# Differential attention in one encoder kernel: both components' scores in one product with the keys on a diagonal, and the product with V turned so that queries lie on partitions

## The chip, the cores and the metric

One core of one Trainium2 chip runs the whole program. The metric is the device time of one execution in microseconds (us); the time of a kernel is the median of its runs.

## What is computed

The reference is a two-layer encoder in float32 on 256 positions of width 2048: a conformer convolution, a gated FFN with a 3-tap convolution, a differential attention, a second FFN, with RMS norms between. The change lies in the attention. For each of 16 heads it does, cut to what matters:

```python
q = q.reshape(B, S, N_HEADS, 2, HEAD_DIM) * (HEAD_DIM ** -0.5)   # two components of 64 channels
k = k.reshape(B, S, N_HEADS, 2, HEAD_DIM)
v = v.reshape(B, S, N_HEADS, 2 * HEAD_DIM)                       # 128 channels
s = einsum('bqhcd,bkhcd->bhcqk', qb, k)                          # scores of each component c
s = where(allowed, s + bias, -inf)                               # by blocks of 128 queries
p = softmax(s)
a = p[:, :, 0] - lam * p[:, :, 1]
o = einsum('bhqk,bkhe->bqhe', a, v)
o = rmsnorm(o, subln_g) * (1 - lambda_init)                      # over the 128 channels of a head
return o.reshape(B, S, D_MODEL) @ w_o
```

The first 128 queries see only the first 128 keys, so one of the four 128 x 128 blocks of a head is never computed.

## The kernel before, in words

**Layout.** Activations lie with channels on the 128 partitions and the 256 positions along the row. A weight block of 128 x 1024 is loaded by SP's queue (`load_w`, L140), split by ACT into a rounded part `hi` (L150) and by DVE or POOL into the rest `lo` (L152). A projection (`pair`, L215) multiplies `hi` with both parts of the activations in one product of 512 columns (L238, at the last channel block L236) and `lo` with the rounded part in one of 256 columns (L239, L235). So a projection is 32 such pairs of products, and PE never stops for anything else. The tile names `pp`, `s`, `t`, `o` are PSUM buffers: two each of `pp` and `s`, one each of `t` and `o`.

**Steps.** The program is a list of steps, one per weight block. `at(n, f)` hangs a piece of work n steps later. A scheduler that builds the program then sets the order on each engine, so the place in the list is where a piece may begin to stand, not where it stands. Each engine works through its own list strictly in order.

**Attention before** (`attention`, L782). Every four heads a group of V products comes first (`v_group`, 96 products of 512 columns, L807 to L809); then each head has its q and k projection, and after it the pieces of that head, each in between the projections of later heads:

- `qk_post` (L826): q and k are summed, normed and each split into `hi` and `lo`; POOL copies the first 128 columns of both, unsplit.
- `scores` (L845): the two components lie on partitions 0 to 63 and 64 to 127. The first query block is two products of 64 rows in full float32 (L851); the second is three split products per component, also of 64 rows (L854). Then the softmax on DVE and ACT (L861 to L873).
- `transp` (L876): three transposes bring keys onto partitions (L879); the first key block is split in two (`AT`), the second kept whole.
- `av` (L885): V is stationary, so the result has channels on partitions: three products of 256 columns and one of 128 in full float32 (L888 to L891).
- `subln` (L899) sums the squares over partitions with products by ones (L286), DVE and POOL make the reciprocal root (L297, L298); `subln2` (L906) spreads it over the partitions with two products (L292), DVE multiplies, and the result is split for the last projection.

After the heads come the projections by `w_o`; the last channel block of the first two is held back until the last head is done.

A full float32 product appears as two records in the trace, a split one as one record.

Of the kernel before, what the change touches and what calls it, by code (L numbers as in the profile page):

```python
# [8 lines left out]
F32 = mybir.dt.float32  # L9
F32R = mybir.dt.float32r  # L10
# [4 lines left out]
P = 128  # L15
S = 256
# [45 lines left out]
class Builder:  # L62
# [683 lines left out]
    def attn_setup(self):  # L746
# [32 lines left out]
        for i in range(2):  # L779
            self.AT.append((self.ph2.tile([P, 2, S], F32R, name=f"at{i}"), self.ph2.tile([P, P], F32, name=f"au{i}")))  # L780

    def attention(self, nin, nout):  # L782
# [3 lines left out]
        V, U, O, BM = {}, {}, {}, {}  # L786

        def v_group(g, off):
            box = {}
            n = c.VK * 512  # L790
            for k0 in range(0, KT, c.VK):
# [3 lines left out]
                def mm(hi, lo, k0=k0):  # L795
                    if k0 == 0:
                        box["ps"] = self.pp.tile([P, 2, 512], F32, tag="pp", name=self.nm("pp"))
                    if k0 == 0:
                        for e in range(4):
                            V[4 * g + e] = self.act_tile()  # L800
# [10 lines left out]
                def post():  # L811
                    for e in range(4):
                        h = 4 * g + e
                        v = V[h][1]
                        U[h] = self.ph2.tile([P, P], F32, tag="vu", name=self.nm("vu"), bufs=6)
                        src = [box["ps"][:, t, e * P:(e + 1) * P] for t in range(2)]
                        r = nin["rc"]
                        nc.scalar.activation(v[:, 0, :P], src[0], AF.Copy, scale=r[:, 0:1])
                        nc.vector.scalar_tensor_tensor(v[:, 1, :P], src[0], r[:, 0:1], v[:, 0, :P].bitcast(F32), ALU.mult,
                                                       ALU.subtract)  # L820
                        nc.scalar.activation(U[h], src[1], AF.Copy, scale=r[:, 1:2])
# [4 lines left out]
        def qk_post(h, ps):  # L826
            t = self.summed(ps)
            nc.vector.tensor_tensor(t, t, nin["rstd"].unsqueeze(1).to_broadcast([P, 2, S]), ALU.mult)
            q = self.b2("Y", F32R)
            k = self.b2("Y", F32R)  # L830
            qk = self.b1("G").rearrange("p (x s) -> p x s", x=2)
# [5 lines left out]
            self.at(2, lambda: scores(h, q, k, qk))  # L837
# [7 lines left out]
        def scores(h, q, k, qk):  # L845
            bm = BM.pop(h)
            ps = [self.psx("s", [P, 2, S]) for _ in range(2)]

            comp = [slice(cc * HD, (cc + 1) * HD) for cc in range(2)]
            for cc, d in enumerate(comp):  # L850
                nc.tensor.matmul(ps[cc][:, 0, :P], qk[d, 0, :], qk[d, 1, :], start=True, stop=True)  # L851
            for i, (qh, kh) in enumerate(((0, 0), (0, 1), (1, 0))):
                for cc, d in enumerate(comp):
                    nc.tensor.matmul(ps[cc][:, 1, :], q[d, qh, P:], k[d, kh, :], start=(i == 0), stop=(i == 2))  # L854
            sm = self.sm.tile([P, 2, 8], F32, tag="smx", name=self.nm("smx"), bufs=2)
            at_ = self.b2("A")
            for t in range(2):
                nk = P * (t + 1)
                s = self.b2("Z")[:, :, :nk]
                for cc in range(2):  # L860
                    nc.vector.scalar_tensor_tensor(s[:, cc, :], ps[cc][:, t, :nk], HD ** -0.5, bm[:, S - nk:], ALU.mult,  # L861
                                                   ALU.add)
# [13 lines left out]
        def transp(h, at_):  # L876
            ps = self.psx("t", [P, 2, S])
            for kt, t in ((0, 0), (0, 1), (1, 1)):
                nc.tensor.transpose(ps[:, kt, t * P:(t + 1) * P], at_[:, t, kt * P:(kt + 1) * P], self.ident)  # L879
            A, B = self.AT[h % 2]  # L880
            self.split_act(A, ps[:, 0, :])
            nc.scalar.copy(B, ps[:, 1, P:])
            self.at(3, lambda: av(h, A, B))

        def av(h, A, B):  # L885
            po = self.psx("t" if h == H - 1 else "o", [P, S])
            v = V[h][1]
            nc.tensor.matmul(po, v[:, 0, :P], A[:, 0, :], start=True, stop=False)  # L888
            nc.tensor.matmul(po[:, P:], U.pop(h), B, start=False, stop=False)
            nc.tensor.matmul(po, v[:, 0, :P], A[:, 1, :], start=False, stop=False)  # L890
            nc.tensor.matmul(po, v[:, 1, :P], A[:, 0, :], start=False, stop=True)  # L891
            self.free([V.pop(h)])
            o = self.b1("O")
            nc.scalar.copy(o, po)
            sq = self.b1("O")
            nc.scalar.activation(sq, po, AF.Square)
            self.at(2, lambda: subln(h, o, sq))

        def subln(h, o, sq):  # L899
            ps = self.psx("t" if h == H - 1 else "o", [P, 4])  # L900
            self.chan_sums(ps, [sq])
            rc = self.c2()
            self.rsqrt_cols(rc, ps[:, 0:4:2], 1.0 / P)
            self.at(2, lambda: subln2(h, o, rc))

        def subln2(h, o, rc):  # L906
            rr = self.psx("t" if h == H - 1 else "o", [P, S])
            self.rows(rr, rc)
            nc.vector.tensor_tensor(o, o, rr, ALU.mult)
            O[h] = self.act_tile()  # L910
            self.split_act(O[h][1], o, self.sg)
# [156 lines left out]
```

## Time and profile before

| | before |
|---|---|
| median of 3 runs | 2267.56 us (2267.46 to 2270.97) |
| the profiled execution, device time | 2268.81 us |
| its span in the profile | 2267.0 us |
| PE busy | 2219.3 us, 98% of the span |
| PE weight loads | 1944.0 us, 86% |
| DVE busy | 1635.4 us, 72% |
| ACT busy | 1205.2 us, 53% |
| POOL busy | 292.0 us, 13% |
| DMA | 417.55 MB, mean 184 GB/s |
| granted clock of PE, whole run | 0.99 of 2.4 GHz |

Engines in the profile: PE multiplies, PEld is its weight load, DVE and ACT work on tiles, POOL is GpSimd, SP issues loads. Matmuls are pipelined, so a record's duration holds latency that overlaps the next one: what a product costs PE is the distance from its start to the next start. That is how PE's prices are read below.

### The profile page before, as it was taken

What the parts mean: (1) busy time and instruction counts of PE and PEld (TensorE: products, weight loads), DVE (VectorE), ACT (ScalarE), POOL (GpSimd) and SP (SyncE); (2) the same over time, 40 slices, a digit from 0 to 9 for tenths busy, and PEclk for the clock granted to TensorE, in tenths of its full rate; (3) what the DMA queues carried; (4) which work ended last, traced back from release to release, by engine and by line L of the source; (5) the groups of instructions that cost most, each with busy time, mean ns of one, the idle gap of its engine ahead of it and who ended that gap; (6) DMA issues with size and microseconds to landing.
All of it is one profiled execution on the core that took longest, in us unless ns stands there. A gap on an engine that the chain in (4) does not pass through costs nothing.

```text
span 2267.0 us, 34768 instructions
## 1 busy us (share of the span) xinstructions
PE 2219.3 (98%) x13382; PEld 1944.0 (86%) x13382; DVE 1635.4 (72%) x2491; ACT 1205.2 (53%) x1788; POOL 292.0 (13%) x197
## 2 busy tenths in 40 slices
PE   5999899999999999999999999999999999999998
PEld 5999788788888888888888888888888888888887
DVE  4788675877767777677777677767777677676774
ACT  4333554655545555555555555555555455554554
POOL 4788510100000000000110101110000000000002
PEclk8999999999999999999999999999999999999999
DMA  6677357755555555555555545455555555555552
GB/s 234 196 215 212 116 192 161 241 185 193 187 191 188 187 186 189 191 187 186 195 167 167 167 161 168 151 196 185 189 186 187 192 187 187 191 187 188 188 189 98
DMA packets 126007, 417.55 MB, mean 184 GB/s; under 512 B 14416, under 2 KB 26704, under 8 KB 125840
## 3 DMA queue, kind: packets, MB, share of 16 engines
q1 hardware_dynamic: 113040, 400.42, 53.9%
q10 hardware_dynamic: 11520, 11.45, 2.0%
q0 software_dynamic: 1280, 3.46, 1.3%
q8 instruction: 105, 1.72, 0.3%
q14 instruction: 62, 0.51, 0.1%
HBM read 407.55 MB, written 7.72 MB: 183 GB/s over the span
## 4 chain that ended last, share of the span: by engine, by line
PE 94%; DMA 2%; DVE 1%; POOL 0%; ACT 0%; issue 0%; ACTq 0%; POOLq 0%; DVEq 0%
PE pp L238 48%; PE pp L239 25%; PE pp L229 7%; PE pp L236 4%; PE pp L235 2%; PE pp L807 1%; PE pp L809 1%; PE pp L808 1%; DMA raw<-in_w_up_dram 1%; PE s L498 1%; DMA R<-ud 0%; PE o L292 0%; PE s L854 0%; DMA ud<-cpad 0%; PE t L498 0%; PE o L286 0%
## 5 line engine op out<-in xcount | busy, mean ns | idle before, releaser
L238 PE MATMUL pp<-act,hi 128*128 128x512 f32 x3902 | 1382.6, 396 | 6.2 <-DVE act L645 3.1
L239 PE MATMUL pp<-act,lo 128*128 128x256 f32 x3902 | 1097.5, 281 | 0.0
L150 ACT CAST hi<-raw 128x1024 fp32r<-128x1024 f32 x752 | 788.0, 1049 | 529.2 <-PE pp L238 180.9
L152 DVE TENSOR_TENSOR lo<-raw,hi 128x1024 fp32r<-128x1024 f32 x686 | 846.0, 1234 | 301.0 <-ACT hi L150 299.0
L238 PEld LDWEIGHTS pp<-act,hi 128*128 128x128 f32 x3902 | 733.8, 188 | 167.4 <-DVE act L645 3.4
L239 PEld LDWEIGHTS pp<-act,lo 128*128 128x128 f32 x3902 | 741.1, 190 | 10.3
L238 PE MATMUL pp<-actb,hi 128*128 128x512 f32 x856 | 306.8, 396 | 1.7 <-ACT hi L150 1.7
L239 PE MATMUL pp<-actb,lo 128*128 128x256 f32 x856 | 240.8, 281 | 0.8 <-DVE lo L152 0.8
L333 POOL TENSOR_TENSOR ssq<-ssq,Z 128x512 f32<-128x512 f32 x24 | 35.6, 1483 | 1516.6 <-ACT Z L329 1516.5
L229 PE MATMUL pp<-act,hi 128*128 128x256 f32 x1088 | 203.4, 289 | 9.1 <-ACT act L279 6.2
L238 PEld LDWEIGHTS pp<-actb,hi 128*128 128x128 f32 x856 | 160.7, 188 | 40.1 <-ACT hi L150 2.0
L229 PEld LDWEIGHTS pp<-act,hi 128*128 128x128 f32 x1088 | 173.7, 196 | 15.6 <-ACT act L279 6.2
L152 POOL TENSOR_TENSOR lo<-raw,hi 128x1024 fp32r<-128x1024 f32 x66 | 158.3, 2414 | 57.6 <-ACT hi L150 52.1
L239 PEld LDWEIGHTS pp<-actb,lo 128*128 128x128 f32 x856 | 162.0, 189 | 1.3 <-DVE lo L152 1.1
L229 PE MATMUL pp<-act,lo 128*128 128x256 f32 x544 | 156.5, 288 | 1.7 <-POOL lo L152 1.5
L382 ACT COPY E<-pp 128x512 f32<-128x512 f32 x109 | 63.9, 586 | 171.5 <-PE pp L236 163.8
L268 DVE TENSOR_TENSOR E<-pp,E 128x512 f32<-128x512 f32 x104 | 71.8, 691 | 105.1 <-ACT E L266 104.9
L266 ACT COPY E<-pp 128x512 f32<-128x512 f32 x104 | 60.8, 585 | 162.7 <-PE pp L236 162.5
L704 DVE SCALAR_TENSOR_TENSOR Y<-fpad,prm,Y 128x256 f32<-128x256 f32 x352 | 146.8, 477 | 0.0
L384 DVE TENSOR_TENSOR x<-pp,x 128x512 f32<-128x512 f32 x101 | 69.7, 690 | 89.5 <-ACT E L382 89.0
L701 ACT ACTIVATE Y<-fpad,prm 128x256 f32<-128x256 f32 x176 | 96.3, 595 | 47.5 <-DVE fpad L697 47.5
L229 PEld LDWEIGHTS pp<-act,lo 128*128 128x128 f32 x544 | 106.7, 196 | 2.1 <-POOL lo L152 1.7
(222 smaller groups left out, 1841.9 us busy)
## 6 DMA issues: line engine op xcount, KB each, us to landing
raw<-in_w_up_dram SPq DMA_DIRECT2D x352, 512.0 KB, 3.9
raw<-in_w_down_dram SPq DMA_DIRECT2D x176, 512.0 KB, 3.9
raw<-in_w_in_dram SPq DMA_DIRECT2D x64, 512.0 KB, 4.4
raw<-in_w_qk_dram SPq DMA_DIRECT2D x64, 512.0 KB, 3.6
raw<-in_w_out_dram SPq DMA_DIRECT2D x32, 512.0 KB, 3.9
raw<-in_w_v_dram SPq DMA_DIRECT2D x32, 512.0 KB, 3.6
raw<-in_w_o_dram SPq DMA_DIRECT2D x32, 512.0 KB, 3.6
R<-ud ACTq DMA_DIRECT2D x52, 132.0 KB, 4.6
```

The source lines that it names most:

```text
L150: nc.scalar.copy(hi[:, :n], raw[:, :n])
L152: ins = eng.tensor_tensor(lo[:, :n], raw[:, :n], hi[:, :n].bitcast(F32), ALU.subtract)
L229: nc.tensor.matmul(ps[:, 0:S], w[:, kk, cs], xt[:, x, :], start=(k == first and n == 0), stop=(k == last and n == 2))
L236: nc.tensor.matmul(*main, start=False, stop=True)
L238: nc.tensor.matmul(*main, start=(k == first), stop=False)
L239: nc.tensor.matmul(*corr, start=False, stop=False)
L266: nc.scalar.copy(cs, ps[:, :, S:])
L268: nc.vector.tensor_tensor(t, ps[:, :, 0:S], cs, ALU.add)
L382: nc.scalar.copy(cs, ps[:, :, S:])
L384: nc.vector.tensor_tensor(x, ps[:, :, 0:S], x, ALU.add)
L701: nc.scalar.activation(y[:, j, :], u[:, j, FK - 1:], AF.Identity, scale=self.col("fw", ch * FK + FK - 1), bias=self.col("fb", ch))
L704: nc.vector.scalar_tensor_tensor(y[:, j, :], u[:, j, q:q + S], self.col("fw", ch * FK + q), y[:, j, :], ALU.mult, ALU.add)
```

## The change

- **Scores.** q keeps its 128 rows (both components). The keys of component 0 go to rows 0 to 63 of a first half-row of `KD`, those of component 1 to rows 64 to 127 of a second half-row; the rest of `KD` is zero, set once by four memsets (L786 of the new text) in `attn_setup`. One product then gives both components side by side. There are three split products for each query block, of 256 and of 512 columns (L863), all with 128 rows. The full-float32 products of the first block and POOL's copy go; the keys' split is now two copies and two subtractions on 64 partitions (L840, L842).
- **Mask and bias** are added for both components in one DVE instruction per query block (two instead of four, L869).
- **V** is kept whole in float32, two heads to a tile; the two evictions of a pair of heads cover both (ACT and DVE one each).
- **Product with V.** The transposed probabilities are copied whole (one ACT copy) and are stationary: three full-float32 products of 128 columns (L898) give queries on partitions.
- **Norm.** Queries are on partitions, so ACT squares and sums along the row (two instructions with accumulation, L903), and DVE scales by a column (two, L910). The products by ones and the spreading products go; two transposes bring the result back (L916).

```diff
+        self.KD = [self.ph2.tile([P, 2, S], F32R, name=f"kd{i}") for i in range(2)]
+        for t in self.KD:
+            for cc in range(2):
+                d = slice((1 - cc) * HD, (2 - cc) * HD)
+                nc.vector.memset(t[d, cc, :].bitcast(F32), 0.0)
...
-            self.split_act(k, t[:, 1, :])
-            nc.gpsimd.tensor_copy(qk, t[:, :, :P])
+            for i in range(2):
+                for cc in range(2):
+                    d = slice(cc * HD, (cc + 1) * HD)
+                    if i == 0:
+                        nc.scalar.copy(self.KD[0][d, cc, :], t[d, 1, :])
+                    else:
+                        nc.vector.tensor_tensor(self.KD[1][d, cc, :], t[d, 1, :], self.KD[0][d, cc, :].bitcast(F32),
+                                                ALU.subtract)
...
-            for cc, d in enumerate(comp):
-                nc.tensor.matmul(ps[cc][:, 0, :P], qk[d, 0, :], qk[d, 1, :], start=True, stop=True)
-            for i, (qh, kh) in enumerate(((0, 0), (0, 1), (1, 0))):
-                for cc, d in enumerate(comp):
-                    nc.tensor.matmul(ps[cc][:, 1, :], q[d, qh, P:], k[d, kh, :], start=(i == 0), stop=(i == 2))
+            for t in range(2):
...
+                nk = P * (t + 1)
+                ps.append(self.psx("s", [P, 2, nk]))
+                for i, (x, k) in enumerate(((0, kh), (0, kl), (1, kh))):
+                    nc.tensor.matmul(ps[t], q[:, x, t * P:(t + 1) * P], k[:, :, :nk], start=(i == 0), stop=(i == 2))
...
+            A = self.AT[h % 2]
+            nc.scalar.copy(A, ps)
+            self.at(3, lambda: av(h, A))
...
+            po = self.psx("o", [P, 2, P])
+            v = V[h // 2][1][:, h % 2, :].rearrange("p (t c) -> p t c", t=2)
+            for i, (kt, t) in enumerate(((0, 0), (0, 1), (1, 1))):
+                nc.tensor.matmul(po[:, t, :], A[:, i, :], v[:, kt, :], start=(kt == 0), stop=(kt == t))
...
+            for t in range(2):
+                nc.scalar.activation(sq[:, t * P:(t + 1) * P], po[:, t, :], AF.Square, accum_out=sums[:, t:t + 1])
+            self.rsqrt_cols(rc, sums, 1.0 / P)
+            self.at(1, lambda: scaled(h, po, rc))
...
+        def scaled(h, po, rc):
+            o = self.b1("O").rearrange("p (t c) -> p t c", t=2)
+            for t in range(2):
+                nc.vector.tensor_scalar(o[:, t, :], po[:, t, :], rc[:, t:t + 1], None, ALU.mult)
+            self.at(2, lambda: back(h, o))
...
+        def back(h, o):
+            ps = self.psx("t", [P, S])
+            for t in range(2):
+                nc.tensor.transpose(ps[:, t * P:(t + 1) * P], o[:, t, :], self.ident)
+            O[h] = self.act_tile()
+            self.split_act(O[h][1], ps, self.sg)
```

The scheduler sets the order anew. Three places of it follow, as the built program lists them; a number behind a name is a buffer's, and "x2" means that the row stands twice. Outside the attention the order changes at one more place only, the first two `w_out` projections after the convolution.

PE, the scores of the fourth head, before: `s` are the two score buffers, `G` POOL's copy, `Y` the split q and k, `pp` the projection between which they stand.

```order
L851 MATMUL s_11805<-G_11735 128x128
L851 MATMUL s_11806<-G_11735 128x128
L292 MATMUL o_11773<-ident,c_11702 128x128 x2
L854 MATMUL s_11805<-Y_11734,Y_11733 128x256
L854 MATMUL s_11806<-Y_11734,Y_11733 128x256
L854 MATMUL s_11805<-Y_11734,Y_11733 128x256
L854 MATMUL s_11806<-Y_11734,Y_11733 128x256
L854 MATMUL s_11805<-Y_11734,Y_11733 128x256
L854 MATMUL s_11806<-Y_11734,Y_11733 128x256
L809 MATMUL pp_11747<-hi_11679,act_10704 128x512
```

and in the change, where L888 is a transpose and L813 to L815 are the V products:

```order
L888 MATMUL t_11767<-ident,A_11630 128x128
L863 MATMUL s_11772<-kd_3983,Y_11709 128x256
L863 MATMUL s_11776<-kd_3983,Y_11709 128x512
L814 MATMUL pp_11722<-lo_11679,act_10763 128x512
L888 MATMUL t_11767<-ident,A_11630 128x128 x2
L815 MATMUL pp_11722<-hi_11678,act_10763 128x512
L863 MATMUL s_11772<-kd_3984,Y_11709 128x256
L863 MATMUL s_11772<-kd_3983,Y_11709 128x256
L863 MATMUL s_11776<-kd_3984,Y_11709 128x512
L863 MATMUL s_11776<-kd_3983,Y_11709 128x512
```

The products with the keys' rounded part stand first, the other four after a few products of the projection.

DVE, at the end of the convolution, where the layer norm's last channel block is made (L523, L569) and its sums are read (L611): one piece of the difference.

```order
 L519 SCALAR_TENSOR_TENSOR pp_2952<-cpad_252,cprm,pp_2952 128x256 x2
 L523 TENSOR_TENSOR O_2983<-pp_2952,O_2983 128x256
+L786 MEMSET kd_3983 64x256 x2
+L786 MEMSET kd_3984 64x256 x2
 L569 TENSOR_TENSOR act_2966<-pp_2952,O_2983 128x256
 L611 SCALAR_TENSOR_TENSOR mom<-o_2989,early 128x4
```

The four memsets that zero `KD` have been moved ahead to this place.

PE, the end of the held projections by `w_o`, before: `pp_14382` is the first of them, whose buffer the next projection `pp_14690` takes over.

```order
L236 MATMUL pp_14382<-act_14373,hi_14219 128x512
L236 MATMUL pp_14467<-act_14373,hi_14445 128x512
L235 MATMUL pp_14467<-act_14373,lo_14446 128x256
L236 MATMUL pp_14467<-act_14373,hi_14445 128x512
L236 MATMUL s_14552<-act_14373,hi_14530 128x512
L236 MATMUL s_14553<-act_14373,hi_14530 128x512
L238 MATMUL pp_14690<-act_11905,hi_14548 128x512
```

and in the change, where the two are `pp_14186` and `pp_14494`:

```order
L236 MATMUL pp_14186<-act_14177,hi_14039 128x512
L236 MATMUL pp_14271<-act_14177,hi_14249 128x512
L235 MATMUL pp_14271<-act_14177,lo_14250 128x256
L236 MATMUL pp_14271<-act_14177,hi_14249 128x512
L238 MATMUL s_14357<-act_14156,hi_14334 128x512
L239 MATMUL s_14357<-act_14156,lo_14335 128x256
L235 MATMUL s_14356<-act_14177,lo_14335 128x256
L236 MATMUL s_14356<-act_14177,hi_14334 128x512
L235 MATMUL s_14357<-act_14177,lo_14335 128x256
L236 MATMUL s_14357<-act_14177,hi_14334 128x512
L238 MATMUL pp_14494<-act_11701,hi_14352 128x512
```

Four more products stand between the end of the first projection and the product that takes its buffer.

## Rows read from the trace of the kernel before

**Rows 1.** The page: engines' busy time; the chain that ended last, by engine.

```profile
PE 2219.3 (98%) x13382; PEld 1944.0 (86%) x13382; DVE 1635.4 (72%) x2491; ACT 1205.2 (53%) x1788; POOL 292.0 (13%) x197
...
PE 94%; DMA 2%; DVE 1%; POOL 0%; ACT 0%; issue 0%; ACTq 0%; POOLq 0%; DVEq 0%
```

**Rows 2.** Attention's stretch: length, busy of PE, PEld, DVE, ACT, POOL, clock, DMA.

```profile
1103.10:1454.40 351.30, 351.23 (x2016) 297.84 (x2015) 250.22 (x514) 195.08 (x399) 36.41 (x33) 1.00 0.51 166
```

**Rows 3.** Timeline of PE, stage marks: start, duration, engine, line, operation, tiles.

```profile
1118.63 0.39 PE L808 MATMUL pp<-lo,act 128*128 128x512 f32 x1
...
1125.91 0.39 PE L238 MATMUL pp<-act,hi 128*128 128x512 f32 x1
...
1137.21 0.39 PE L238 MATMUL pp<-act,hi 128*128 128x512 f32 x1
...
1176.73 0.40 PE L807 MATMUL pp<-hi,act 128*128 128x512 f32 x1
...
1256.44 0.40 PE L807 MATMUL pp<-hi,act 128*128 128x512 f32 x1
```

**Rows 4.** Timeline of PE around the sums by ones and the product with V.

```profile
1206.49 0.50 PE L286 MATMUL o<-ones,O 128*128 128x2 f32 x4
...
1207.17 0.28 PE L239 MATMUL pp<-act,lo 128*128 128x256 f32 x1
...
1210.47 0.28 PE L888 MATMUL o<-at,act 128*128 128x256 f32 x1
...
1211.05 0.39 PE L238 MATMUL pp<-act,hi 128*128 128x512 f32 x1
```

**Rows 5.** Chain that ended last: two transposes and the spreading products; start, length.

```profile
1421.87 0.22 PE t L879 x2
1422.09 0.45 PE o L292 x4
```

**Rows 6.** Timeline of PE around the scores of two heads.

```profile
1143.91 0.40 PE L238 MATMUL pp<-act,hi 128*128 128x512 f32 x1
1144.24 0.49 PE L851 MATMUL s<-G 64*128 64x128 f32 x4
...
1145.24 0.39 PE L238 MATMUL pp<-act,hi 128*128 128x512 f32 x1
...
1223.13 0.39 PE L238 MATMUL pp<-act,hi 128*128 128x512 f32 x1
1223.45 0.49 PE L851 MATMUL s<-G 64*128 64x128 f32 x4
...
1223.99 0.71 PE L292 MATMUL o<-ident,c 128*128 128x128 f32 x4
...
1225.49 0.50 PE L854 MATMUL s<-Y,Y 64*128 64x256 f32 x4
...
1226.15 0.40 PE L238 MATMUL pp<-act,hi 128*128 128x512 f32 x1
```

**Rows 7.** Groups by line: DVE's subtraction in the split of q and k.

```profile
L276 DVE TENSOR_TENSOR Y<-E,Y 128x256 fp32r<-128x256 f32 x32 | 12.3, 420 | 0.0
```

**Rows 8.** One memset; timeline and busy time by stretch at the layer norm.

```profile
L400 DVE MEMSET ones<- x1: 165/165/165, 0.8 to 0.8; 128x128 f32 x1
...
254.24 0.42 DVE L569 TENSOR_TENSOR act<-pp,O 128x256 f32<-128x256 f32 x1
...
262.11 0.80 PE L238 MATMUL pp<-act,hi 128*128 128x512 f32 x1 [3.09 <-DVE act L645]
...
262.00:270.00 8.00, 7.89 (x29) 6.81 (x30) 7.33 (x16) 6.27 (x16) 6.00 (x5) 0.62 0.00 1
```

**Rows 9.** Timeline of PE at the end of the held projections.

```profile
1455.87 0.64 PE L236 MATMUL s<-act,hi 128*128 128x512 f32 x2
1456.85 0.50 PE L238 MATMUL pp<-act,hi 128*128 128x512 f32 x1 [0.34 <-DVE x L384]
```

**Rows 10.** Groups by line, attention's stretch: POOL's reciprocal root.

```profile
L298 POOL TENSOR_TENSOR c<-c,mhalf 128x2 f32<-128x2 f32 x16 | 17.6, 1102 | 130.6 <-DVE c L297 122.1 <-DVE smx L865 8.5
```

More of the change, by code (lines that the diff above doesn't have):

```diff
@@ L797, in mm @@
                         box["ps"] = self.pp.tile([P, 2, 512], F32, tag="pp", name=self.nm("pp"))
-                    if k0 == 0:
-                        for e in range(4):
-                            V[4 * g + e] = self.act_tile()
+                        for e in range(0, 4, 2):
+                            V[(4 * g + e) // 2] = self.act_tile(F32)
                     for kk in range(c.VK):
@@ L811, in post @@
                 def post():
[L812 to L821, printed above, removed]
+                    for e in range(0, 4, 2):
+                        v = V[(4 * g + e) // 2][1].rearrange("p a (t c) -> p a t c", t=2)
+                        for t in range(2):
+                            src = box["ps"][:, t, e * P:(e + 2) * P].rearrange("p (a c) -> p a c", a=2)
+                            r = nin["rc"][:, t:t + 1]
+                            if t == 0:
+                                nc.scalar.activation(v[:, :, t, :], src, AF.Copy, scale=r)
+                            else:
+                                nc.vector.tensor_scalar(v[:, :, t, :], src, r, None, ALU.mult)
                 self.step(w, n, 512, mm, post=post if k0 + c.VK >= KT else None)
@@ L859, in scores @@
                 s = self.b2("Z")[:, :, :nk]
-                for cc in range(2):
-                    nc.vector.scalar_tensor_tensor(s[:, cc, :], ps[cc][:, t, :nk], HD ** -0.5, bm[:, S - nk:], ALU.mult,
-                                                   ALU.add)
+                nc.vector.scalar_tensor_tensor(s, ps[t], HD ** -0.5, bm[:, S - nk:].unsqueeze(1).to_broadcast([P, 2, nk]),
+                                               ALU.mult, ALU.add)
                 mx = sm[:, t, 0:2]
@@ L876, in transp @@
         def transp(h, at_):
[L877 to L909, printed above, removed]
+            ps = self.psx("t", [P, 3, P])
+            for i, (kt, t) in enumerate(((0, 0), (0, 1), (1, 1))):
+                nc.tensor.transpose(ps[:, i, :], at_[:, t, kt * P:(kt + 1) * P], self.ident)
@@ new lines, in transp, with av @@
+            A = self.AT[h % 2]
+            nc.scalar.copy(A, ps)
+            self.at(3, lambda: av(h, A))
+        def av(h, A):
+            po = self.psx("o", [P, 2, P])
+            v = V[h // 2][1][:, h % 2, :].rearrange("p (t c) -> p t c", t=2)
+            for i, (kt, t) in enumerate(((0, 0), (0, 1), (1, 1))):
+                nc.tensor.matmul(po[:, t, :], A[:, i, :], v[:, kt, :], start=(kt == 0), stop=(kt == t))
+            if h % 2:
+                self.free([V.pop(h // 2)])
+            sq, sums, rc = self.b1("O"), self.c2(), self.c2()
+            for t in range(2):
+                nc.scalar.activation(sq[:, t * P:(t + 1) * P], po[:, t, :], AF.Square, accum_out=sums[:, t:t + 1])
+            self.rsqrt_cols(rc, sums, 1.0 / P)
+            self.at(1, lambda: scaled(h, po, rc))
@@ L910, in subln2 @@
+        def scaled(h, po, rc):
[5 more added lines that the diff above has]
+            ps = self.psx("t", [P, S])
+            for t in range(2):
+                nc.tensor.transpose(ps[:, t * P:(t + 1) * P], o[:, t, :], self.ident)
             O[h] = self.act_tile()
-            self.split_act(O[h][1], o, self.sg)
+            self.split_act(O[h][1], ps, self.sg)
```

15 lines of the change are left out of this document (7 added, 8 removed).

## The prediction

> **What bounds the kernel now.** I read the page first. PE is busy 98% of the span and 94% of the chain that ended last runs over it; DVE is next with 72% [rows 1]. The mean over the run could hide a stage with another limit, so the second view is the busy time of attention's own stretch: PE is busy for 351.23 of 351.30 us at a granted clock of 1.00, the upper of its two levels (2.4 GHz), while DVE is busy for 250 us, ACT for 195 and POOL for 36 [rows 2]. So PE sets the pace here and has no gap to give back. What the change is worth in this stage is how many nanoseconds of PE it removes, unless it makes PE wait. The two other places that it touches, the layer norm after the convolution and the end of the held projections, do have idle time on PE, and there the question is the opposite one: what PE waits for.
>
> Records of PE overlap, so prices are distances between starts. Between 1118.63 and 1125.91 stand 32 V products and nothing else: 7.28 / 32 = 0.2275 us each. From 1125.91 to 1137.21 runs the first head's projection, 32 pairs, with nothing between: 11.30 us, 0.353 a pair [rows 3]. Four heads repeat as one period, V group to V group: 1256.44 - 1176.73 = 79.71 us [rows 3]. Of this the 96 V products take 21.84 and four projections 45.20. The rest, 12.67 us or **3.17 us a head**, is what the small products of attention cost PE. All of it lies on the path.
>
> **The change part by part: PE in attention.** What that rest is made of:
> - The sums by ones: from 1206.49 to 1207.17 is 0.68, less one projection product of 512 columns (0.235, two thirds of a pair) is 0.45 [rows 4]. The spreading products: 0.45 [rows 5]. Both go.
> - The product with V: 1211.05 - 1210.47 = 0.58; three of its products have 256 columns (a third of a pair, 0.118 each), which leaves 0.225 for the one in full float32 [rows 4].
> - Three transposes at 0.11 (two take 0.22) [rows 5]: 0.33.
> - Scores, by difference: 3.17 - 0.45 - 0.45 - 0.58 - 0.33 = 1.36.
>
> The score rows show why 1.36 is a mean. Where all ten records stand together they take 1145.24 - 1143.91 = 1.33 less one pair, 0.98. Where the scheduler has put full-height work between them (spreading products, two projection products), the stretch from 1223.13 to 1226.15 is 3.02; less the spreading (0.45) and two pairs (0.70) the scores take 1.87 [rows 6]. The L851 that follows a full-height product at 1223.13 starts 0.32 later, not 0.235 [rows 6]: each change between 64 and 128 rows leaves a hole on PE that counts as busy.
>
> After the change: the scores are three products of 256 and three of 512 columns, all 128 rows high, which is three projection pairs in shape: 3 x 0.353 = 1.06, wherever they stand. The product with V is three full-float32 products: 3 x 0.225 = 0.68. Five transposes: 0.55. Together 2.29. Saved: 3.17 - 2.29 = 0.88 a head, **14.1 us** in 16. The method is a difference of large numbers: 1% of a projection is 0.11 us a head, so I keep 12.3 to 15.9.
>
> One rule speaks against this edit. Two products of 64 rows in different halves of the array may run side by side; if they did so at full gain, the old scores would cost one full-float32 pair (0.225) and three split pairs (0.118 each), 0.58 in all, and not 1.36. Then the new ones, which multiply by zeros in half of the array, would lose 0.48 a head. The rows give 0.98 at best [rows 6]. The Trainium skill states it in "TensorEngine Tiling (Array Packing)", section Overview, under "Theoretical Speedup": a contraction of at most 64 may gain up to twofold. By that sentence alone the trade would be a loss; the trace does not show the gain at these sizes.
>
> **What is off the path.** Key split: one more subtraction on DVE and one more copy on ACT a head, on half the partitions but as long a row; I take 0.42 each [rows 7], 6.7 us in all, against 101 us in which DVE is idle here [rows 2]. The mask in two instructions, V's evictions in fewer, one copy of the probabilities instead of a split, POOL's copy gone, squares with accumulation and two scalings instead of one square and one multiplication: these go together, roughly level on DVE and ACT, hidden by PE's products. If that cover failed, PE would show gaps that it does not have now. No DMA is added; weights still arrive at a DMA share of 0.51 [rows 2].
>
> **The memsets.** They are not in attention: the scheduler put all four between L523 and L569, and L569 starts a serial chain (sums, root, normalization) at whose end PE waits, idle for 3.09 us until 262.11 [rows 8]. Everything behind L569 moves by what they take. A memset of 128 columns takes 0.165 [rows 8]; theirs have 256, so 0.165 to 0.33 each. I take 0.25, **+1.0 us** (0.66 to 1.3). PE's clock is low here, a mean of 0.62 from 262 to 270, between 1.2 and 2.4 GHz [rows 8]: a longer idle could stretch the low part, which is a rival below.
>
> **The end of the held projections.** Two products start at 1455.87 and the next at 1456.85: 0.98 where two products need 0.47, so 0.51 is lost waiting for DVE to free the buffer (L384) [rows 9]. In the changed order 0.59 us more of products stands between the end of that buffer's projection and the product that wants it (three pairs instead of two products). I take **-0.5 us** (-0.5 to 0).
>
> **Sum.** -14.1 + 1.0 - 0.5 = -13.6 us. Against the profiled execution of 2268.81 that is 2255.2; the median of the runs lies 1.25 lower, so 2254.0. Its own range, from the bounds: -15.9 + 0.66 - 0.5 = -15.7 and -12.3 + 1.3 = -11.0, that is 2251.8 to 2256.6.
>
> **The rivals.**
> - *The second half of the scores waits for the keys.* In the changed order only two transposes and two products may stand between the products with the rounded keys and those with the rest, and `KD` exists once. If the extra subtraction is late each time, PE waits 0.42 [rows 7] a head, 6.7 us: 2260.7. For it: DVE's list is strict. Against: before, the same chain (sum, norm, split) fed scores without a gap [rows 2].
> - *The low clock lasts longer.* If the stretch at a mean of 0.62 [rows 8] lasted twice as long, 8 us more, 0.38 of it would be lost, 3.0 us: 2257.0. For it: the clock is low just there [rows 8]. Against: only 1 us is added to an idle that already exceeds 3.
> - *Products of 64 rows are cheap.* If 0.58 were the old scores' true price and the rest of the 1.36 belonged to neighbours that stay, 0.78 a head of the saving would be gone: 0.10 x 16 = 1.6 us, less the two small terms, 2266.5, no change that can be told. Against: the measured 0.98 and 1.87 [rows 6]. It is the rule of the Trainium skill's page on tiling, named above.
> - *Slower: DVE's list is blocked.* DVE's scaling (L910) needs POOL's root (L298), and stands directly behind the instruction that feeds POOL (L297) in 7 of the 16 heads. POOL takes 1.10 on average [rows 10]; with the scaling itself, about 0.42 for 256 columns [rows 7], what is queued behind, above all the weights' `lo` parts (L152), is 1.52 late. If PE felt all of it in every head, 16 x 1.52 = 24.3 us turn -13.6 into +10.7: 2278.3. It decides from 13.6 / 16 = 0.85 us a head. Against: weights are split four steps ahead (L186), and a step of eight pairs is 2.8 us; DVE idles for 29% of the stretch [rows 2].
>
> That the change does not do what it says is excluded by the built order, which lists six score products, three with V and five transposes a head.
>
> **How the numbers follow.** Forecast 0.71, late keys 0.12, low clock 0.07, cheap 64-row products 0.06, blocked DVE 0.04. The likeliest gives 2254.0. The range reaches from 2251 to 2261, over the low clock and the late keys; it leaves out 0.10 for the last two and some 0.08 of the forecast's own tails. A measurement tells about 0.2%, 4.5 us. Faster by more: 0.71 + 0.12 + 0.07 = 0.90; same: 0.06; slower: 0.04.
>
> **What would show it.** In the profile after: a period of four heads near 76.2 us (79.71 - 4 x 0.88); score products a third of a pair and two thirds of one from start to start; PE still without gaps between V groups and at clock 1.00; L569 later by about 1 us against L523; no wait for L384 at the end. The forecast is wrong if PE waits at L863, if its new products cost more than their shapes say, or if the time goes in the layer norm.

## The result, and the profile after

The changed kernel takes 2255.12 us in the median (2252.66 to 2257.02, 4 runs), the kernel before, beside it on the same chip, 2267.86 (2267.46 to 2270.97, 4 runs). The ratio is 0.9940, with a 95% interval of 0.9923 to 0.9957: 12.7 us faster, where 2254.0 (2251 to 2261) was predicted. The profiled execution took 2254.46, with a span of 2252.7 against 2267.0 before, so the two traces lie 14.3 us apart.

The page of the changed kernel, which answers to [rows 1]: busy time of each engine, and the chain that ended last by engine.

```profile
PE 2205.2 (98%) x13238; PEld 1937.4 (86%) x13238; DVE 1634.2 (73%) x2471; ACT 1200.7 (53%) x1796; POOL 273.5 (12%) x181
...
PE 94%; DMA 2%; DVE 0%; issue 0%; ACT 0%; POOL 0%; ACTq 0%; POOLq 0%; DVEq 0%
```

PE is still what bounds the kernel. It has lost 14.1 us of busy time, practically the whole difference of the spans. Busy time by stretch says where, in the columns of [rows 2]: attention from its first V product to the end of the last projection before the held ones.

```profile
1103.70:1439.40 335.70, 335.70 (x1868) 289.77 (x1868) 247.32 (x490) 191.11 (x407) 17.97 (x17) 1.00 0.56 174
```

PE is busy for all of the 335.70 us, at the upper level of its clock, and the list of waits of PE in this stretch is empty. DVE and ACT changed by 3 and 4 us and remain far below PE; POOL's part halved. Nothing took PE's place.

The stage marks on PE, which answer to [rows 3], are the first product of the second and third group of V products:

```profile
1176.07 0.40 PE L813 MATMUL pp<-hi,act 128*128 128x512 f32 x1
...
1251.96 0.40 PE L813 MATMUL pp<-hi,act 128*128 128x512 f32 x1
```

Four heads now take 75.89 us instead of 79.71: 3.82 less, 0.955 a head, where 0.88 was predicted (period 76.2). From the norm ahead of attention to the norm behind it (in both PE spreads a norm's root with L292, and the distance is taken between these starts) the trace shows 393.11 us instead of 408.99, 15.9 less: 16 x 0.955 = 15.3, and the wait at the end that is gone. Of this, 0.6 us (net) was paid ahead of attention and 0.9 behind it, which leaves the 14.3 of the spans.

New scores and new product with V, on PE's timeline:

```profile
1221.95 0.40 PE L238 MATMUL pp<-act,hi 128*128 128x512 f32 x1
1222.19 0.86 PE L863 MATMUL s<-kd,Y 128*128 128x256 f32 x4
1222.89 0.28 PE L239 MATMUL pp<-act,lo 128*128 128x256 f32 x1
...
1241.40 0.28 PE L239 MATMUL pp<-act,lo 128*128 128x256 f32 x1
1241.52 0.83 PE L898 MATMUL o<-act,at 128*128 128x128 f32 x6
1242.10 0.47 PE L238 MATMUL pp<-act,hi 128*128 128x512 f32 x1
```

Four of the six score products (two of 256 columns, two of 512; a row of several records names the first one's shape) stand between 1222.19 and 1222.89: 0.70, which is two projection pairs [rows 3], as predicted from their shapes. The other two take one pair, 0.35, so the scores cost 1.05 a head (1.06 predicted). Compare [rows 6]: the full-height product behind them starts without a hole. The product with V takes 0.58 between starts, and the projection product behind it is stretched by some 0.1 (0.47 against 0.39); taken to the start of the second product behind it, it costs 0.67 on average over the four heads of the period (0.68 predicted).

The groups by line, as in [rows 7] and [rows 10] (DVE's and ACT's part of the keys' split, DVE's scaling, POOL's root):

```profile
L842 DVE TENSOR_TENSOR kd<-E,kd 64x256 fp32r<-64x256 f32 x32 | 13.3, 415 | 0.5
...
L910 DVE TENSOR_SCALAR O<-o,c 128x128 f32<-128x128 f32 x32 | 9.7, 346 | 8.4 <-POOL c L298 8.3
```

```profile
L840 ACT CAST kd<-E 64x256 fp32r<-64x256 f32 x32 | 13.0, 405 | 0.4
```

```profile
L298 POOL TENSOR_TENSOR c<-c,mhalf 128x2 f32<-128x2 f32 x16 | 16.3, 1019 | 300.0 <-DVE c L297 300.0
```

The subtraction on 64 partitions takes as long (415 ns) as that on 128 (420, [rows 7]). And DVE does stand and wait for POOL's root ahead of its scaling, as the slower rival had it: 8.3 us in all, 11 times in the list of waits. PE felt none of it.

At the layer norm, DVE's timeline and PE's first projection product behind it, which answer to [rows 8]:

```profile
253.19 0.42 DVE L523 TENSOR_TENSOR O<-pp,O 128x256 f32<-128x256 f32 x1
253.72 1.36 DVE L786 MEMSET kd<- 64x256 f32 x4
255.01 0.35 DVE L569 TENSOR_TENSOR act<-pp,O 128x256 f32<-128x256 f32 x1
...
263.23 0.80 PE L238 MATMUL pp<-act,hi 128*128 128x512 f32 x1 [3.10 <-DVE act L645]
```

From L523 to L569 it is now 1.82 us; before it was 0.46 (L523 stood at 253.78 there, L569 at 254.24 [rows 8]). The memsets cost 1.36 where 1.0 was predicted. From L523 to the first product it is 10.04 instead of 8.33.

At the end of the held projections, which answers to [rows 9], the wait for L384 is gone:

```profile
1441.72 0.39 PE L236 MATMUL s<-act,hi 128*128 128x512 f32 x1
1441.95 0.43 PE L238 MATMUL pp<-act,hi 128*128 128x512 f32 x1
```

The two products start 0.23 apart, which is the time of one product: the 0.5 us is saved as predicted.

### The profile page after: what moved, and what is told of

Same layout as the page of the kernel before. It is cut to its first block, busy times and chain, and to the rows that moved or that the text cites. A ratio compares the mean times of both kernels' runs of the same rounds, so it can differ in the third digit from the quotient of the medians.

```text
span 2252.7 us, 34458 instructions
## 1 busy us (share of the span) xinstructions
PE 2205.2 (98%) x13238; PEld 1937.4 (86%) x13238; DVE 1634.2 (73%) x2471; ACT 1200.7 (53%) x1796; POOL 273.5 (12%) x181
## 4 chain that ended last, share of the span: by engine, by line
PE 94%; DMA 2%; DVE 0%; issue 0%; ACT 0%; POOL 0%; ACTq 0%; POOLq 0%; DVEq 0%
PE pp L238 48%; PE pp L239 25%; PE pp L229 7%; PE pp L236 4%; PE pp L235 2%; PE pp L813 1%; PE pp L815 1%; PE pp L814 1%; DMA raw<-in_w_up_dram 1%; PE s L863 1%; PE s L498 1%; PE o L898 0%; DMA R<-ud 0%; PE t L498 0%; PE s L507 0%; DMA ud<-cpad 0%
## 5 line engine op out<-in xcount | busy, mean ns | idle before, releaser
L239 PE MATMUL pp<-act,lo 128*128 128x256 f32 x3902 | 1095.7, 281 | 0.0
L150 ACT CAST hi<-raw 128x1024 fp32r<-128x1024 f32 x752 | 788.1, 1049 | 532.2 <-PE pp L238 186.2
L239 PEld LDWEIGHTS pp<-act,lo 128*128 128x128 f32 x3902 | 739.4, 189 | 10.2
L239 PE MATMUL pp<-actb,lo 128*128 128x256 f32 x856 | 241.3, 282 | 0.8 <-DVE lo L152 0.8
L239 PEld LDWEIGHTS pp<-actb,lo 128*128 128x128 f32 x856 | 162.6, 190 | 1.2 <-DVE lo L152 1.1
L382 ACT COPY E<-pp 128x512 f32<-128x512 f32 x109 | 63.9, 586 | 170.7 <-PE pp L236 163.0
L384 DVE TENSOR_TENSOR x<-pp,x 128x512 f32<-128x512 f32 x101 | 69.8, 691 | 87.8 <-ACT E L382 87.4
```

Of the source, the lines that this page charges most:

```text
L150: nc.scalar.copy(hi[:, :n], raw[:, :n])
L239: nc.tensor.matmul(*corr, start=False, stop=False)
L382: nc.scalar.copy(cs, ps[:, :, S:])
L384: nc.vector.tensor_tensor(x, ps[:, :, 0:S], x, ALU.add)
```

## The experiments

The question left open was why a head saved 0.955, and which part of the change it comes from. The theory of the prediction: PE's small products became fewer or cheaper, term by term. Its rivals: the gain is that of one part alone; or it is only a matter of the order in which the products of 64 rows stand, and the diagonal isn't needed. Three runs look at the memsets. Each ratio is to the kernel before on the same chip; the period of four heads is read from V group to V group, which excludes what happens elsewhere.

| run | median us | ratio to before, 95% interval | period us | norm to norm us |
|---|---|---|---|---|
| before | 2267.86 | | 79.71 | 408.99 |
| the change | 2255.12 | 0.9923 to 0.9957 | 75.89 | 393.11 |
| turned_alone | 2258.99 | 0.9939 to 0.9972 | 77.73 | 400.02 |
| scores_only | 2262.55 | 0.9963 to 0.9986 | 78.07 | 403.14 |
| together | 2269.16 | 0.9995 to 1.0014 | 78.90 | 408.62 |
| together2 | 2264.50 | 0.9970 to 0.9988 | 78.48 | 403.72 |
| turned_together | 2253.59 | 0.9923 to 0.9948 | 75.73 | 393.45 |
| pinned | 2254.14 | 0.9924 to 0.9953 | 75.90 | 393.11 |
| late_zero | 2253.80 | 0.9924 to 0.9948 | 75.89 | 393.11 |
| after_again | 2255.01 | 0.9930 to 0.9957 | 75.89 | 393.33 |

### turned_alone: the new product with V and the new norm, old scores

Against the change: no `KD`, no memsets, scores as before.

```diff
-            for i in range(2):
-                for cc in range(2):
...
+            k = self.b2("Y", F32R)
+            qk = self.b1("G").rearrange("p (x s) -> p x s", x=2)
+            self.split_act(k, t[:, 1, :])
+            nc.gpsimd.tensor_copy(qk, t[:, :, :P])
```

> The change with the scores left as they were before (64-row products, keys split on DVE and ACT, POOL's copy; no KD, no memsets): V, the product with V and the norm are as in the change. Theory A (the parts add up on PE, scores 1.36 to 1.06 us a head): sums by ones and spreading 0.90 a head gone, product with V 0.10 dearer, two transposes 0.22 more, so the period of four heads is 79.71 - 4 x 0.58 = 77.4 us, up to 77.8 because the built order breaks the old score products a little more often; against 75.9 in the change. Total about 2259 to 2261: 4 x 1.5 to 1.9 above the change, less some 1.1 for the missing memsets. Rival C (the old scores were cheap and all of the gain is the norm's): period 75.9, total about 2254.

```profile
1177.35 0.48 PE L808 MATMUL pp<-hi,act 128*128 128x512 f32 x1
...
1234.98 0.28 PE L239 MATMUL pp<-act,lo 128*128 128x256 f32 x1
1235.19 0.49 PE L851 MATMUL s<-G 64*128 64x128 f32 x4
1235.43 0.37 PE L854 MATMUL s<-Y,Y 64*128 64x256 f32 x2
1235.73 0.50 PE L238 MATMUL pp<-act,hi 128*128 128x512 f32 x1
1236.07 0.28 PE L239 MATMUL pp<-act,lo 128*128 128x256 f32 x1
...
1236.88 0.40 PE L238 MATMUL pp<-act,hi 128*128 128x512 f32 x1
1237.21 0.50 PE L854 MATMUL s<-Y,Y 64*128 64x256 f32 x4
1237.64 0.39 PE L239 MATMUL pp<-act,lo 128*128 128x256 f32 x1
1237.86 0.39 PE L238 MATMUL pp<-act,hi 128*128 128x512 f32 x1
...
1255.08 0.48 PE L808 MATMUL pp<-hi,act 128*128 128x512 f32 x1
```

The period is 1255.08 - 1177.35 = 77.73: this part alone saves 1.98 a period, 0.495 a head (0.58 would follow from the prediction's terms: 0.45 + 0.45 + 0.58 + 0.33 before, 0.68 + 0.55 after). So neither part is the whole gain. The rows, PE's timeline of one head, show why the old scores are dear. They stand in two groups. The first runs from the L239 at 1234.98 to the second product behind it at 1236.07, 1.09, less the two projection products themselves (0.117 + 0.235): 0.74. The second likewise from 1236.88 to 1237.86: 0.98 - 0.35 = 0.63. Together 1.37, for the ten records that take 0.98 where they stand in one group [rows 6]. Over the four heads of this period the scores come to 1.50 a head, in two or three groups each, against 1.38 counted in the same way before and 1.05 with the diagonal.

### together and together2: the kernel before with its score products in one group

Only the numbers of steps after which a piece may begin. In together all heads have them; together2 leaves the last four heads as they were and moves the sums by ones too.

```diff
-            self.at(2, lambda: scores(h, q, k, qk))
+            self.at(3 if h < 12 else 2, lambda: scores(h, q, k, qk))
...
-            self.at(4, lambda: transp(h, at_))
+            self.at(5 if h < 12 else 4, lambda: transp(h, at_))
...
-            self.at(3, lambda: av(h, A, B))
+            self.at(4 if h < 12 else 3, lambda: av(h, A, B))
...
-            self.at(2, lambda: subln(h, o, sq))
+            self.at(3 if h < 12 else 2, lambda: subln(h, o, sq))
```

> The kernel before with three delays one step longer (scores 2 to 3, transposes 4 to 5, product with V 3 to 4), nothing else: every product is the same, but the built order now keeps the ten score products of three heads in four together and breaks those of the fourth once. Theory A (each change between 64 and 128 rows leaves a hole on PE): scores fall from 0.98 + 1.37 + 1.31 + 1.87 to 3 x 0.98 + 1.37 a period, so the period is 79.71 - 1.22 = 78.5 us and the time 2263. Rival B (the height does not matter, a score product costs what it costs and the old order's 1.87 is other work): period 79.7, time 2267.9. Later pieces could also make PE wait at the end of the heads; then the period shows 78.5 and the total does not.

Its median is that of the kernel before. The period did fall, to 78.90, but norm to norm only 0.4 us were gained: from the fourth V group to the norm behind attention it takes 193.4 us, where the kernel before takes 190.5. The last heads' pieces now come too late for the end. PE's three longest waits in this kernel, from the first V product on (what waited, for what, total, times, longest), are ones that the kernel before and the change don't have:

```profile
PE pp L238 <- DVE act L280: 1.5, 2, 1.2
PE o L888 <- DVE c L297: 0.8, 3, 0.3
PE t L292 <- POOL c L298: 0.5, 1, 0.5
```

So the attempt did not answer its question, and together2 mends it.

> As together, but the sums by ones come one step later too (2 to 3), and the four delays are the old ones for the last four heads, so that the end of the heads is as in the kernel before. Still the same products as before the change. Built order: all four heads of the first three periods have their ten score products together but one, which is broken once. Theory A: period 79.71 - 1.26 = 78.45 us, no wait of PE for the sums' inputs, and the time 3 x 1.26 = 3.8 us below before, about 2264. Rival B (height does not matter): period 79.7, time 2268.

```profile
1175.81 0.39 PE L807 MATMUL pp<-hi,act 128*128 128x512 f32 x1
...
1254.29 0.39 PE L807 MATMUL pp<-hi,act 128*128 128x512 f32 x1
```

The period is 78.48, 1.23 less than before, PE waits nowhere in attention, and the interval of the ratio lies below 1. In this period three of the four heads have their ten score products in one group; in the fourth the spreading products still stand among them. The same products, of the same number and shape, thus cost 0.31 us a head less, and nearly all of it lies in the scores: counted as in turned_alone, they take 1.10 a head instead of 1.38. That work of full height among the products of 64 rows costs PE time is thus shown, and not only read from single rows. Products of 128 rows don't pay this price: the diagonal's scores take 0.35 and 0.70 in two groups, one projection pair and two.

### turned_together: the turned part with the old scores in one group

turned_alone, with the first three edits of together2.

> The change with the old 64-row scores (as turned_alone), and the delays of the first twelve heads one step longer for scores, transposes and product with V, so that in the built order the ten score products of every head stand together; no KD, no memsets. Theory A: a score of ten products together costs 0.98 a head against 1.05 for the six products with keys on a diagonal, so the period is 75.9 - 4 x 0.07 = 75.6 us and the time 1.4 (memsets) and some 0.8 (scores of twelve heads) below the change, about 2253: the diagonal is not needed once the height changes are few. Rival D (the diagonal itself, not the height changes, brings the scores' part): period 77.7 as in turned_alone, time 2259.

```profile
1172.15 0.47 PE L808 MATMUL pp<-hi,act 128*128 128x512 f32 x1
...
1230.43 0.28 PE L239 MATMUL pp<-act,lo 128*128 128x256 f32 x1
1230.64 0.49 PE L851 MATMUL s<-G 64*128 64x128 f32 x4
1230.89 0.60 PE L854 MATMUL s<-Y,Y 64*128 64x256 f32 x6
1231.42 0.50 PE L238 MATMUL pp<-act,hi 128*128 128x512 f32 x1
1231.76 0.28 PE L239 MATMUL pp<-act,lo 128*128 128x256 f32 x1
...
1247.88 0.47 PE L808 MATMUL pp<-hi,act 128*128 128x512 f32 x1
```

The period is 75.73, 0.16 below that of the change, and norm to norm it is level with it (393.45; the last four heads still have their scores in several groups). The median, 2253.59, is the lowest of the study, though its interval overlaps with that of the change. So the diagonal is not what makes the scores cheap. What the change did with 128 rows can be had with 64 rows if they stand together: 1.33 from 1230.43 to 1231.76 less one pair is 0.98, against 1.05 on the diagonal.

The rows also correct the prediction. Singly, the trace has the six L854 starting in pairs, 0.01 apart within a pair, at 1230.89, 1231.09 and 1231.21: the last pair comes 0.11 after the one before, which is what one full-height product of 256 columns takes. The two components' products do run side by side. The kernel before shows the same, so it could have been read ahead of the change: in the group of ten in [rows 6], too, the last pair starts 0.11 after the one before. One after another at the prediction's prices, the ten would take 2 x 0.225 + 6 x 0.118 = 1.16, and they take 0.98.

### scores_only: the diagonal with the old product with V and the old norm

```diff
+        self.KD = [self.ph2.tile([P, 2, S], F32R, name=f"kd{i}") for i in range(2)]
...
+                ps.append(self.psx("s", [P, 2, nk]))
+                for i, (x, k) in enumerate(((0, kh), (0, kl), (1, kh))):
+                    nc.tensor.matmul(ps[t], q[:, x, t * P:(t + 1) * P], k[:, :, :nk], start=(i == 0), stop=(i == 2))
```

> The old product with V and the old norm, with the new scores on diagonal keys alone; to make room the two-component tiles Y have two buffers instead of four (the convolution uses them too, so only attention's period is compared). Theory A: what the scores cost depends on what the scheduler puts among them. Counted between neighbouring projection products they take 1.38 us a head in the kernel before and 1.50 with the turned part alone; the new ones take 1.05. Then this part saves 0.33 a head by itself, a period of about 78.3 us (79.71 - 4 x 0.33 = 78.4, up to 0.2 less for the neighbours). Theory B: the two parts simply add, so this one is worth the 1.84 a period that the turned part leaves of the whole: 77.9. If the new scores cost more where the old norm's full-height products stand among them, it lies above 78.5.

```profile
1173.70 0.39 PE L813 MATMUL pp<-hi,act 128*128 128x512 f32 x1
...
1251.77 0.39 PE L813 MATMUL pp<-hi,act 128*128 128x512 f32 x1
```

The period is 78.07, between the two expectations (78.2 to 78.4, and 77.9): neither is confirmed as stated. The diagonal alone saves 1.64 a period, the turned part alone 1.98, 3.62 together, and both at once 3.82. They very nearly add; 0.05 a head comes only with both. The old scores' growth from 1.38 to 1.50 in turned_alone points the same way, but is 0.12, so the two are not reconciled.

### pinned, late_zero and after_again: the memsets

pinned fixes the memsets' place in `attn_setup`; late_zero has them in the first head's `bias` instead.

```diff
-                nc.vector.memset(t[d, cc, :].bitcast(F32), 0.0)
+                self.tc.keep_in_program_order(nc.vector.memset(t[d, cc, :].bitcast(F32), 0.0))
```

> The change with the four memsets pinned in the order of the program (behind what DVE was given before the first FFN), so that they no longer stand between L523 and L569. Theory M (the memsets delay a serial chain and, through PE's low clock, a little more): from the start of L523 to PE's first w_out product 8.3 us as before the change, instead of 10.04, and the run 1.1 to 1.7 us shorter (2253.6), hardly to be told in the time, plainly in the trace. Rival (the layer norm was longer for another reason, such as the clock alone): the stretch stays at 9.5 or more with the memsets gone from it.

The edit missed its aim: the memsets still stood between L523 and L569, 1.82 apart as before. It serves as a second execution of the change (2254.14).

```diff
         def bias(h):
+            if h == 0:
+                for t in self.KD:
+                    for cc in range(2):
+                        d = slice((1 - cc) * HD, (2 - cc) * HD)
+                        self.tc.keep_in_program_order(nc.vector.memset(t[d, cc, :].bitcast(F32), 0.0))
```

> The change with the four memsets moved to the first head's projection, where DVE has idle time (pinned and the change have them between L523 and L569, so pinned moved nothing). Theory M: from L523 to L569 0.46 us as before instead of 1.82; from L569 to PE's first w_out product between 7.9 and 9.1, by when PE's clock falls and not by this edit; the run 1.4 us shorter than the change, about 2253.7, at the edge of what can be told. Rival: something else fills the place and L569 stays late.

> The change itself, beside the others on the same chip: 2255, with L523 to L569 1.82 us and a period of 75.9 us, and L569 to PE's first w_out product anywhere from 7.9 to 9.1 (8.2 in its first profile, 9.0 in pinned, whose order there is the same).

after_again is the change itself, unedited, beside late_zero. L569 to PE's first product is 9.04 in it, at the upper end of what was expected. DVE's timeline in late_zero, with the four memsets gone from the layer norm:

```profile
252.25 0.42 DVE L523 TENSOR_TENSOR O<-pp,O 128x256 f32<-128x256 f32 x1
252.71 0.42 DVE L569 TENSOR_TENSOR act<-pp,O 128x256 f32<-128x256 f32 x1
```

L523 to L569 is 0.46 again, and PE's first product comes 8.29 behind L523, as before the change (8.33). The memsets now stand in attention, at 1127.7 to 1129.1, ahead of the period, and cost nothing there: from norm to norm it is 393.11, as in the change. The medians, 2253.80 and 2255.01 on one chip, lie 1.2 apart in the direction expected, with overlapping intervals; the price at the place is shown by the trace, not by the times.

The memsets have a second price that the prediction doesn't have. After the layer norm, PE waits once more in the change, for ACT's part of a weight split:

```profile
289.16 0.47 PE L238 MATMUL pp<-act,hi 128*128 128x512 f32 x1 [1.09 <-ACT hi L150]
```

The same wait of 1.1 us stands in the change, after_again, pinned and scores_only, all of which have the memsets at the layer norm (between L523 and L569, in scores_only just ahead of L523), and in none of before, late_zero, turned_alone, turned_together, together and together2. The wait is made by the order of the first two `w_out` projections, the one place outside attention where the order changes. ACT's timeline shows it, first in the change, then in late_zero:

```profile
287.51 0.59 ACT L382 COPY E<-pp 128x512 f32<-128x512 f32 x1 [3.62 <-PE pp L236]
288.00 1.05 ACT L150 CAST hi<-raw 128x1024 fp32r<-128x1024 f32 x1
```

```profile
284.20 0.59 ACT L382 COPY E<-pp 128x512 f32<-128x512 f32 x1 [2.66 <-PE pp L236]
284.68 1.05 ACT L150 CAST hi<-raw 128x1024 fp32r<-128x1024 f32 x1
```

The split L150 that PE waits for stands in ACT's list behind L382, which takes a finished projection out of PSUM. In the four kernels with the memsets at the layer norm, the last products (L235, L236) of the first two projections stand in one group, so L382 comes later and ACT idles 3.5 to 3.6 us for it; in the other six they stand in two groups, with other products between them, and ACT idles 2.7. The weights themselves are there: the load that this L150 needs had landed at 280.25. late_zero differs from the change only in the place of the memsets, so the order follows from that place. Of both prices part is given back where PE waits for other inputs anyway, around 395 to 427 us: those 150 products take 31.4 to 32.3 us in the four kernels with the memsets there, 33.6 to 35.7 in five without (32.2 in turned_together, so not all of it is theirs). From L523 to the end of that stretch the change takes 173.9, before 172.6 and late_zero 172.6, 1.3 less. But over all ten traces the distance is 171.2 to 174.2 with the memsets there and 170.5 to 174.8 without, so a net price of the memsets cannot be told.

The rest of the layer norm varies by itself. From L569 to PE's first product it is 7.87 before, 8.22 with the change and 9.03 in pinned; the change itself, executed again, has 9.04. The same stretch by the granted clock (0.50 is 1.2 GHz, the lower level; 1.00 is 2.4 GHz), in three kernels:

```profile
254.24:258.00 3.76, 1.66 (x13) 1.61 (x14) 1.13 (x6) 0.42 (x2) 1.61 (x3) 0.98 0.03 5
258.00:262.11 4.11, 1.02 (x6) 0.72 (x5) 2.07 (x6) 2.07 (x6) 1.69 (x2) 0.50 0.01 2
```

```profile
255.01:258.00 2.99, 1.03 (x8) 0.97 (x8) 0.84 (x5) 0.42 (x1) 0.71 (x1) 0.92 0.04 6
258.00:263.23 5.23, 2.08 (x8) 1.78 (x8) 2.30 (x8) 2.07 (x6) 1.70 (x3) 0.50 0.00 2
```

```profile
254.30:258.00 3.70, 1.84 (x8) 1.78 (x8) 0.83 (x5) 0.42 (x1) 0.61 (x1) 0.50 0.03 5
258.00:263.33 5.33, 2.07 (x8) 1.78 (x8) 2.30 (x8) 2.06 (x6) 1.80 (x3) 0.50 0.00 2
```

The first is the kernel before, the second the change, the third pinned. Where the clock falls before L569's chain, as in pinned, the sums by ones in it run at the lower level and the chain is longer. All ten traces fall in line: the stretch takes 9.04 to 9.11 where the clock falls ahead of L569 or at most 0.6 us behind it (four traces), 8.22 to 8.29 where it falls 1.7 to 2.5 behind (three), and 7.83 to 7.88 where it falls 3.6 to 3.7 behind (three). It needs no memsets: together2 and turned_alone, which have none there, are among the four long ones (9.54 and 9.56 from L523), and together2's code up to attention is that of the kernel before. Why the clock falls earlier in some executions stays open.

## Why the prediction was right

**The bound.** That PE's nanoseconds are the whole price in attention held in every run: a period fell by what PE's products lost, and in the change PE has no wait there.

**The saving a head.** Predicted 0.88, measured 0.955, which makes 15.3 us in 16 instead of 14.1, well within the 12.3 to 15.9 kept. Each new term was right within 0.01 where it can be read: scores 1.05 (1.06), product with V 0.67 (0.68). Counted between neighbouring projection products, the small products of a period fell from 12.7 to 9.1, 0.90 a head; the remaining 0.05 lies in the projections around them and isn't assigned. Split by part, the scores were undervalued: predicted 0.30 a head (1.36 - 1.06), measured 0.41 alone and 0.46 on top of the turned part. The turned part was overvalued: predicted 0.58, measured 0.495 alone and 0.545 on top of the diagonal. The two errors partly cancel, which is luck. The step that was off is "scores, by difference: 1.36", taken as a price that stays. As a mean of the kernel before it holds (1.38 counted), but it is no property of the products: it is one of what the scheduler puts among them, and changes when the neighbours change (1.50 with the turned part alone). That explains the 0.46 on top of the turned part (1.50 - 1.05); of the 0.41 alone it explains 0.33, and 0.08 stays open.

**The memsets.** Predicted +1.0, measured +1.36 at the place itself, above the upper end of 1.3: the price was taken from the width of the row, and the four start 0.36 apart on half the partitions. The step also left something out: with the memsets at that place the order of the first two `w_out` projections is another, ACT takes the first one's result later, and PE waits another 1.1 for the split behind it. The waits near 400 us take part of both back; by before and late_zero the net is 1.3, which lies within the variation of that stretch.

**The end of the held projections.** Predicted -0.5, and the wait is gone.

**The sum.** With the measured terms, and 1.3 for what before and the change differ by from L523 to the end of the stretch near 400 us, -15.3 + 1.3 - 0.5 = -14.5, and the spans differ by 14.3. That this is so close has some luck in it: 0.6 were gained ahead of L523 and 0.9 lost behind attention, both in instructions that the change doesn't touch.

**The rivals.** *Late keys*: in the changed kernel DVE waits for the scores (3.4 us in all) and not PE for the keys; refuted. *The low clock lasts longer*: its mechanism is there, but smaller and not tied to the change; the stretch varies by 0.8 us between two executions of the change and by 1.3 over all ten traces, not by 3. *Cheap 64-row products*: its time, 2266.5, is refuted, but the argument against it was only half right. The prediction held that the trace doesn't show the gain. It does, in turned_together and already in the kernel before: the pairs start together, the last one 0.11 after the one before, and ten records take 0.98 where one after another they would take 1.16. The Trainium skill's "TensorEngine Tiling (Array Packing)", section Overview, under "Theoretical Speedup", gives up to twofold for a contraction of at most 64; the last pair, 0.11 for two products, agrees. What the rows give in addition is the price of coming and going: 0.98 measured for one group against 0.58 at full gain is 0.40, and a second group (1.37 against 0.98) costs 0.39 more. So 64-row products are worth having in one group, and lose their gain if they are broken into two. Had the old scores stood in one group from the beginning, the diagonal would have lost about 0.07 a head. *Blocked DVE*: the wait exists (8.3 us, at most 0.9 at a time by the list of waits), but weights are split far enough ahead, and PE never saw it.

## What to carry to other kernels

Where an engine is busy for the whole of a stage, price an edit by distances between starts on that engine, with the neighbours included: a group of products costs its shapes plus what it costs to enter and leave it. Before rewriting the mathematics so that all products have one height, try to move the short ones together: here three changed numbers and the turned product with V gave the same time as the diagonal. And see where the scheduler puts setup work; four memsets of zeros landed in a place where PE was waiting for DVE, and changed the order of products there too.

## What was not expected of the hardware

- Each group of 64-row products between full-height ones cost PE 0.37 to 0.40 us that counts as busy: the full-height product behind it takes 0.34 to the next start instead of 0.235, and the first short one starts some 0.1 late (1230.64, where 1230.43 + 0.117 is 1230.55); the rest lies within the group. What of it is due to the height stays open: behind L898, all of full height, the next product too takes 0.31 to the next start.
- DVE's memset of 256 columns on 64 partitions took 272 ns, and the four started 0.36 apart; one of 128 columns on 128 partitions took 165 [rows 8]. A subtraction on 64 partitions took as long as on 128 (415 and 420 ns): in these rows the length of a row, not the number of partitions, sets DVE's time.
- PE's granted clock fell from 1.00 to 0.50 at different moments of the same stretch in executions with the same instructions: 8.22 and 9.04 us from L569 to PE's first product in two executions of the change.
